# A recurrent layer's loads, decayed scores and state products re-arranged in a four-layer transformer kernel

## The chip, the core and the metric

The kernel runs on one core of a Trainium2 chip. The metric is device time in microseconds (us) for the whole program, which is all four layers in one launch. TensorE is called PE below, VectorE DVE, ScalarE ACT, GpSimd POOL, and SyncE (which here only issues transfers) SP.

## What is computed

Four layers act on 1024 latent tokens and 256 context tokens of width 1024. Layers 0 and 3 are windowed attention, layer 1 is a latent attention, and layer 2, the only one the change touches, is an mLSTM: a gated linear recurrence with a matrix state, run forwards and backwards, with 4 heads, keys of 128 and values of 256. In chunks of 128 tokens (10 chunks for each head and direction) the reference does:

```
c_new = a * c_prev + bb * c_loc
s_qk = einsum('bhctd,bhcsd->bhcts', q, k) * exp(log_d - m_t[..., None])
num = (einsum('bhcts,bhcsv->bhctv', s_qk, v)
       + a_t[..., None] * einsum('bhcvk,bhctk->bhctv', c_st, q))
den = sum(s_qk, axis=-1) + a_t * einsum('bhck,bhctk->bhct', n_st, q)
out = num / maximum(abs(den), exp(-m_t))[..., None]
```

The two directions are added, gated with a sigmoid and a silu, normalized by head and projected.

## The kernel before

Nearly all matrix products are made of 4-byte numbers split in two: `split` writes a rounded high half (`hi`, by ACT or DVE) and the rest (`lo`, by POOL or DVE), and a product then takes three PE instructions (high by high, high by low, low by high). A product whose operands are left as plain 4-byte floats is one instruction in the program; the trace shows two for it.

Layer 2 runs in stages (`layer_c`). First come the queries and keys of each head. Then twelve weight chunks of 256 columns are worked off in the loop over `c`. Chunks 0 to 3 give the values (`vd`), 4 to 7 the output gate (`sgd`), and 8 to 11 the second gate (`gzd`). The first eight chunks cover ten tiles of 128 tokens; the last four cover six, since the first four tiles of the second gate are put off (`late_z`). That makes 104 tiles. A tile is 24 products of 256 columns into a buffer `n`, which ACT, DVE or POOL empty into a small tile (`v` or `sg`) that SP stores.

Two generators are advanced inside this loop, so many steps for each tile. `gate_rows` computes the decay rows from the gates (on 36 partitions, a long chain on DVE, ACT and POOL) and stores them to `rmd` and `cqd`. `decays` then works through 24 groups of up to four chunks (4 heads, 2 directions): it loads five tiles a group (`e`, `a`, `q`, `st`, `kt`), and stores three results, the scaled keys `ked`, the decayed scores `gdd` and the scaled queries `qad`, up to 256 KB each.

After the loop come 40 steps, one for each head and chunk. Values of a head are loaded from `vd` as high and low halves (`rv`) by `load_head`; `load_decay` loads `ked`, `qad` and `gdd` two groups ahead and `group` splits them. In each step `state` makes the next state `cs` and `chunk` makes the output; the split of the state (`ch`, `cl`) lies between them. Between these products `fill(n)` puts `n` pieces of three products of `late_z`, 128 pieces in all. The tiles of the last head's steps feed the output projection (`wo`), whose weights are split in the last steps.

A scheduler with a simulated timeline sets the order of each engine's instructions; on the chip each engine and each queue, SP's too, takes its own in that order.

Of the kernel before, what the change touches and what calls it, by code (L numbers as in the profile page):

```python
# [9 lines left out]
F32 = mybir.dt.float32  # L10
F32R = mybir.dt.float32r
BF16 = mybir.dt.bfloat16
AF = mybir.ActivationFunctionType
ALU = mybir.AluOpType
# [9 lines left out]
NTL = NLAT // 128  # L24
# [7 lines left out]
def as32(ap):  # L32
    return ap.bitcast(F32)
# [31 lines left out]
class Dit:  # L65
# [1331 lines left out]
    def layer_c(self, i, hpool, hT, hs):  # L1397
        nc, ins, P = self.nc, self.ins, self.P
# [229 lines left out]
        rows = iter(())  # L1628
# [11 lines left out]
        def load_head(h):  # L1640
            sp = slots[h % 2]
            vv = []
            for x in range(2):
                v = sp.tile([128, NT, 258], F32R, name=f"rv{x}", bufs=1)
                nc.sync.dma_start(out=as32(v[:, :, 0:256]),
                                  in_=vd[x, :, h * 256:(h + 1) * 256].rearrange("(t p) d -> p t d", p=128))
                if x == 1:
                    nc.gpsimd.memset(as32(v[:, :, 256:258]), 0.0)
                else:
                    nc.gpsimd.memset(as32(v[:, :, 256:257]), 1.0)  # L1650
                    nc.gpsimd.memset(as32(v[:, :, 257:258]), -1.0)
                vv.append(v)
            hsum = sp.tile([128, NT, 256], F32, name="hsum", bufs=1)
            heads[h] = dict(v=vv, hsum=hsum, seen=set(), st=[None, None], nx=[None, None])

# [96 lines left out]
        dec = iter(())  # L1752
        for c in range(12):
            kind, h = c // 4, c % 4
            w = self.need(P["voz", c])
            tiles = [t for t in ORDER if kind < 2 or t >= 4]
            go = self.pacer(len(tiles), P["voz", c + 1] if c < 11 else None)
            if kind == 2:
                ghr = head_gain(wt, h)
            for t in tiles:  # L1760
                p = self.psn()
                self.proj_tok(p[:, 0:256], hT, t, w, 256)
                if pend and (c or t == 2):
                    kt_sT(*pend)
                    pend = None
                p = p[:, 0:256]
                go()
                r, cc = slice(t * 128, t * 128 + 128), slice(h * 256, h * 256 + 256)
                if kind == 0:
                    v = wt.tile([128, 2, 256], F32R, name="v", bufs=2)  # L1770
                    self.split(v[:, 0], v[:, 1], p, "act", "dve")
                    nc.sync.dma_start(out=vd[:, r, cc].rearrange("x p d -> p x d"), in_=as32(v))
                elif kind == 1:
                    s = wt.tile([128, 256], F32, name="sg", bufs=3)
                    nc.scalar.activation(out=s, in_=p, func=AF.Tanh, scale=0.5)
                    nc.vector.tensor_scalar(out=s, in0=s, scalar1=1.0, scalar2=0.5, op0=ALU.add, op1=ALU.mult)
                    nc.sync.dma_start(out=sgd[r, cc], in_=s)
                else:
                    gate_z(wt, p, t, h, ghr)
                next(rows, None)  # L1780
                for _ in range(2 if kind == 2 else 1):
                    next(dec, None)
            if c == 0:
                p1.release()
                gw = self.pool("gw", os_)
                rows = gate_rows()
            elif c == 6:
                for _ in rows:
                    pass
                gw.release()  # L1790
                pg = self.pool("pg", os_)
                dec = decays(pg)
# [30 lines left out]
        def fill(n):  # L1823
            for _ in range(n):
                next(zs, None)
# [3 lines left out]
        slots = [None, self.pool("slotb", os_)]  # L1829
        slots[0] = self.pool("slota", os_)  # L1830
        load_head(0)
        load_head(1)
        G, QA, KE = {}, {}, {}

        dec_t = {}
# [1 line left out]
        def load_decay(n):  # L1837
            if n < len(keys):
                h, d, c0 = keys[n]
                m = min(4, NT - c0)  # L1840
                dec_t[keys[n]] = []
                for src in (ked, qad, gdd):
                    x = p2.tile([128, 4, 128], F32, name="dT", bufs=9)
                    nc.sync.dma_start(out=x[:, 0:m].rearrange("p c t -> p (c t)"),
                                      in_=src[h, d, :, c0 * 128:(c0 + m) * 128])
                    dec_t[keys[n]].append(x)

        def group(h, d, c0):

            m = min(4, NT - c0)  # L1850
            load_decay(keys.index((h, d, c0)) + 2)
            ke, qa, dT = dec_t.pop((h, d, c0))
            for src, dic, nm in ((ke, KE, "k"), (qa, QA, "a"), (dT, G, "g")):
                hi = p2.tile([128, 4, 128], F32R, name=nm + "hi", bufs=3)
                lo = p2.tile([128, 4, 128], F32R, name=nm + "lo", bufs=3)
                self.split(hi[:, 0:m], lo[:, 0:m], src[:, 0:m], "act", "pool")
                for x in range(m):
                    dic[h, d, c0 + x] = (hi[:, x], lo[:, x])

        def state(h, c):  # L1860

            H = heads[h]
            cn = p2.tile([128, 2, 258], F32, name="cs", bufs=2)
            for d in range(2):
                v = [x[:, toks[d][c], :] for x in H["v"]]
                kh, kl = KE.pop((h, d, c))
                p = self.psn()[:, 0:258]
                self.mm(p, kh, v[0], True, False)
                self.mm(p, kh, v[1], False, False)
                self.mm(p, kl, v[0], False, True)  # L1870
                if c == 0:
                    nc.vector.tensor_copy(cn[:, d], p)
                else:
                    nc.vector.scalar_tensor_tensor(out=cn[:, d], in0=H["st"][0][:, d], in1=p, op0=ALU.mult, op1=ALU.add,
                                                   scalar=consts["abc"][:, 32 * d + h, c:c + 1])
            H["nx"] = (cn, p2.tile([128, 2, 258], F32R, name="ch", bufs=2), p2.tile([128, 2, 258], F32R, name="cl", bufs=2))

        def chunk(h, c):
            H = heads[h]
            w = self.psw()[:, :].rearrange("p (d n) -> p d n", d=2)  # L1880
            tk = [toks[d][c] for d in range(2)]
            for d in range(2):
                v = [x[:, tk[d], :] for x in H["v"]]
                gh, gl = G.pop((h, d, c))
                qh, ql = QA.pop((h, d, c))
                o = w[:, d, 0:258]
                self.mm(o, gh, v[0], True, False)
                self.mm(o, gh, v[1], False, False)
                self.mm(o, gl, v[0], False, c == 0)
                if c:  # L1890
                    _, ch_, cl_ = H["st"]
                    self.mm(o, qh, ch_[:, d], False, False)
                    self.mm(o, ql, ch_[:, d], False, False)
                    self.mm(o, qh, cl_[:, d], False, True)
            if c < NT - 1:
                cn, ch2, cl2 = H["st"] = H["nx"]
                self.split(ch2, cl2, cn, "act", "dve")
            dn = p2.tile([128, 2], F32, name="dn", bufs=3)
            nc.vector.tensor_reduce(out=dn, in_=w[:, :, 256:258], op=ALU.max, axis=AX.X)
            for d in range(2):  # L1900
                nc.vector.tensor_scalar(out=dn[:, d:d + 1], in0=dn[:, d:d + 1], scalar2=None, op0=ALU.max,
                                        scalar1=consts["colq"][:, c, 2 + d, h:h + 1])
            nc.vector.reciprocal(out=dn, in_=dn)
            if tk[0] in H["seen"]:
                for d in range(2):
                    hs_ = H["hsum"][:, tk[d]]
                    nc.vector.scalar_tensor_tensor(out=hs_, in0=w[:, d, 0:256], scalar=dn[:, d:d + 1], in1=hs_,
                                                   op0=ALU.mult, op1=ALU.add)
                    nc.sync.dma_start(out=gd[tk[d] * 128:tk[d] * 128 + 128, h * 256:(h + 1) * 256], in_=hs_)
            else:  # L1910
                for d in range(2):
                    nc.scalar.activation(out=H["hsum"][:, tk[d]], in_=w[:, d, 0:256], func=AF.Copy, scale=dn[:, d:d + 1])
                H["seen"].update(tk)
# [34 lines left out]
        for s, (h, c) in enumerate(steps):  # L1948
# [7 lines left out]
                            group(*key)  # L1956
            if c < NT - 1:
                state(h, c)
                fill(3)
            chunk(h, c)  # L1960
            fill(2)
            if c == 1 and h >= 1:
                if h < 3:
                    load_head(h + 1)
# [119 lines left out]
```

## Time and profile before

| | |
|---|---|
| median of three timed runs | 3041.59 us (3039.66 to 3044.81) |
| the profiled execution | 3034.74 us |
| its span, first to last instruction | 3033.0 us |
| PE busy over the span | 2820.0 us (93%) |
| mean granted PE clock | 0.973 |
| loop over the twelve chunks, first value store to last gate store | 1766.7 to 2137 us |
| 40 recurrent steps, first product to the output projection | 2149.2 to 2308 us |

PE's busy time counts a matmul from its start to its modelled end, and neighbours overlap, so a busy PE can still have room. The number of products in a stretch, times the distance between the starts of two that follow without a wait, says more.

### The profile page before, as it was taken

What the parts mean: (1) busy time and instruction counts of PE and PEld (TensorE: products, weight loads), DVE (VectorE), ACT (ScalarE), POOL (GpSimd) and SP (SyncE); (2) the same over time, 40 slices, a digit from 0 to 9 for tenths busy, and PEclk for the clock granted to TensorE, in tenths of its full rate; (3) what the DMA queues carried; (4) which work ended last, traced back from release to release, by engine and by line L of the source; (5) the groups of instructions that cost most, each with busy time, mean ns of one, the idle gap of its engine ahead of it and who ended that gap; (6) DMA issues with size and microseconds to landing.
All of it is one profiled execution on the core that took longest, in us unless ns stands there. A gap on an engine that the chain in (4) does not pass through costs nothing. (4 is left out here: it accounts for less than half of the span.)

```text
span 3033.0 us, 49504 instructions
## 1 busy us (share of the span) xinstructions
PE 2820.0 (93%) x17344; PEld 2448.9 (81%) x17344; DVE 1664.0 (55%) x3527; ACT 1273.3 (42%) x2685; POOL 1329.4 (44%) x1567
## 2 busy tenths in 40 slices
PE   6999999899989999999898999997798989999898
PEld 4888888678878788888787899997686778888777
DVE  5356666655422566666457645344587743666662
ACT  2245655543311455555333323232454422555662
POOL 4555565545661011000454232245685446655652
PEclk8999999999999999999999999998899999999999
DMA  8455463733355211111444354698886546434433
GB/s 266 150 160 165 131 178 109 227 122 125 95 189 170 58 39 36 33 37 33 137 146 124 115 165 137 202 295 270 258 257 229 186 127 185 125 113 139 150 94 112
DMA packets 460347, 446.36 MB, mean 147 GB/s; under 512 B 38882, under 2 KB 393722, under 8 KB 460098
## 3 DMA queue, kind: packets, MB, share of 16 engines
q1 hardware_dynamic: 455504, 440.40, 46.6%
q8 instruction: 138, 2.26, 0.3%
q10 hardware_dynamic: 4162, 2.14, 0.3%
q0 software_dynamic: 432, 0.66, 0.1%
q14 instruction: 111, 0.91, 0.1%
HBM read 308.19 MB, written 135.53 MB: 146 GB/s over the span
## 5 line engine op out<-in xcount | busy, mean ns | idle before, releaser
L104 DVE TENSOR_TENSOR pl<-n,ph 128x512 fp32r<-128x512 f32 x488 | 327.4, 686 | 139.2 <-ACT ph L95 121.1
L95 ACT ACTIVATE ph<-n 128x512 fp32r<-128x512 f32 x488 | 283.9, 596 | 213.3 <-PE n L90 168.7
L87 PE MATMUL n<-ph,v 128*128 128x256 f32 (+1 forms) x992 | 293.3, 338 | 21.0 <-ACT ph L95 15.2
L921 DVE CUSTOM_DVE_ANT_0 p<-w,mask,nsink 128x640 f32<-128x640 f32 (+2 forms) x288 | 225.0, 805 | 145.8 <-PE w L87 109.2
L87 PE MATMUL n<-wh,hh 128*128 128x256 f32 x960 | 277.8, 289 | 25.7 <-DVE sg L1748 19.7
L90 PE MATMUL n<-ident,p 128*128 128x128 f32 x1952 | 291.9, 276 | 4.3 <-ACT p L1291 1.4
L923 ACT ACTIVATE p<-p,nm 128x641 f32<-128x641 f32 (+2 forms) x288 | 220.7, 768 | 140.6 <-DVE nm L921 111.8
L87 PE MATMUL n<-wl,hh 128*128 128x256 f32 x960 | 274.9, 286 | 3.1 <-DVE wl L104 3.1
L87 PE MATMUL n<-wh,hl 128*128 128x256 f32 x960 | 274.4, 286 | 0.0
L90 PEld LDWEIGHTS n<-ident,p 128*128 128x128 f32 x1952 | 236.6, 142 | 38.5 <-ACT p L1288 2.8
L930 POOL TENSOR_SCALAR p<-p,rl 128x640 f32<-128x640 f32 (+2 forms) x288 | 211.0, 745 | 114.4 <-DVE rl L928 110.2
L87 PE MATMUL n<-pl,v 128*128 128x512 f32 (+1 forms) x656 | 239.1, 365 | 7.8 <-DVE pl L104 6.6
L1339 POOL TENSOR_TENSOR o<-o,z 128x256 f32<-128x256 f32 x40 | 30.3, 757 | 441.6 <-ACT o L1338 266.8
L87 PEld LDWEIGHTS n<-wh,hh 128*128 128x128 f32 x960 | 187.0, 195 | 29.8 <-DVE sg L1748 20.8
L87 PEld LDWEIGHTS n<-ph,v 128*128 128x128 f32 x992 | 175.1, 190 | 40.6 <-ACT ph L95 24.6
L87 PE MATMUL w<-ks,qT 128*128 128x256 f32 (+1 forms) x1088 | 198.3, 309 | 2.1 <-DVE nm L921 1.1
L87 PEld LDWEIGHTS n<-wl,hh 128*128 128x128 f32 x960 | 187.2, 195 | 3.9 <-DVE wl L104 3.8
L87 PEld LDWEIGHTS w<-ks,qT 128*128 128x128 f32 x1088 | 174.1, 189 | 18.8 <-DVE nm L921 4.6
L87 PEld LDWEIGHTS n<-wh,hl 128*128 128x128 f32 x960 | 186.9, 195 | 0.0
L104 POOL TENSOR_TENSOR wl<-raw,wh 128x1024 fp32r<-128x1024 f32 x42 | 105.8, 2524 | 152.4 <-DVE wh L97 142.2
L87 PEld LDWEIGHTS n<-pl,v 128*128 128x128 f32 x656 | 125.4, 191 | 26.9 <-DVE pl L104 18.4
L87 PE MATMUL n<-hh,wh 128*128 128x512 f32 (+1 forms) x336 | 124.4, 370 | 4.8 <-DVE mod L402 4.8
(349 smaller groups left out, 7449.0 us busy)
## 6 DMA issues: line engine op xcount, KB each, us to landing
raw<-in_l_w_ada_dram SPq DMA_DIRECT2D x96, 512.0 KB
raw<-in_l_w_in_dram SPq DMA_DIRECT2D x80, 512.0 KB
qT<-qd SPq DMA_DIRECT2D x576, 64.0 KB
raw<-in_l_w_out_dram SPq DMA_DIRECT2D x32, 512.0 KB
vd<-v SPq DMA_DIRECT2D x60, 256.0 KB
xd<-xt SPq DMA_DIRECT2D x30, 512.0 KB
od<-o SPq DMA_DIRECT2D x112, 128.0 KB
go<-od SPq DMA_DIRECT2D x28, 512.0 KB
```

The costliest lines, as they stand in the source:

```text
L87: self.nc.tensor.matmul(out, lhsT, rhs, start=start, stop=stop)
L90: self.nc.tensor.transpose(out, in_, self.ident)
L95: nc.scalar.activation(out=out, in_=in_, func=AF.Copy)
L104: e.tensor_tensor(out=lo, in0=src, in1=as32(hi), op=ALU.subtract)
L921: nc.vector.tensor_tensor_reduce(out=p[:, 0:n], in0=ps[:, s0:768], in1=mask[:, mo:mo + n], scale=1.0, scalar=sink, op0=ALU.add, op1=ALU.mi ...
L923: nc.scalar.activation(out=p[:, 0:n + 1], in_=p[:, 0:n + 1], func=AF.Exp, scale=-1.0, bias=nm[:, j:j + 1], accum_out=lsum[:, j:j + 1])
L930: nc.gpsimd.tensor_scalar(out=pr[y][:, 0:n], in0=pr[y][:, 0:n], scalar1=rl[:, y:y + 1], scalar2=0.5, op0=ALU.mult, op1=ALU.mult)
L1339: nc.gpsimd.tensor_tensor(out=o, in0=o, in1=z, op=ALU.mult)
```

## The change

It has five parts, all in layer 2. (1) `gate_rows` is advanced by two steps a tile and `decays` by one step throughout (before: one, and one or two); the scratch of `gate_rows` is freed after chunk 3 instead of 6, and `decays` begins from there. (2) The values of a head are loaded in pairs of tiles, ten transfers of 256 KB in the order in which the steps need them, in place of two of 1280 KB; the second head's are loaded at step 2. (3) 24 pieces of `late_z` stand ahead of the first step, then two pieces and one or two follow in each step (before: three and two). (4) The scaled queries are not split, and neither is the state; their product is one of plain 4-byte floats, in place of three. (5) The loaded tiles `dk`, `dq`, `dg` have buffers of their own (3, 4 and 3; before nine shared, `dT`), since `dq` is now held until its last chunk; `cs` has three.

```diff
@@ load_head
-                nc.sync.dma_start(out=as32(v[:, :, 0:256]),
-                                  in_=vd[x, :, h * 256:(h + 1) * 256].rearrange("(t p) d -> p t d", p=128))
...
+            for t in (NTL, 0, NTL - 2, 2, 4):
+                for x in range(2):
+                    nc.sync.dma_start(out=as32(vv[x][:, t:t + 2, 0:256]),
+                                      in_=vd[x, t * 128:(t + 2) * 128, h * 256:(h + 1) * 256]
+                                      .rearrange("(t p) d -> p t d", p=128))
@@ loop over the chunks
-                next(rows, None)
-                for _ in range(2 if kind == 2 else 1):
-                    next(dec, None)
+                for _ in range(2):
+                    next(rows, None)
+                next(dec, None)
...
-            elif c == 6:
+            elif c == 3:
...
         load_head(0)
-        load_head(1)
+        fill(24)
@@ load_decay
-                for src in (ked, qad, gdd):
-                    x = p2.tile([128, 4, 128], F32, name="dT", bufs=9)
+                for src, nm in ((ked, "dk"), (qad, "dq"), (gdd, "dg")):
+                    x = p2.tile([128, 4, 128], F32, name=nm, bufs=4 if nm == "dq" else 3)
@@ group
-            for src, dic, nm in ((ke, KE, "k"), (qa, QA, "a"), (dT, G, "g")):
+            for x in range(m):
+                QA[h, d, c0 + x] = qa[:, x]
+            for src, dic, nm in ((ke, KE, "k"), (dT, G, "g")):
@@ chunk
                 if c:
-                    _, ch_, cl_ = H["st"]
-                    self.mm(o, qh, ch_[:, d], False, False)
-                    self.mm(o, ql, ch_[:, d], False, False)
-                    self.mm(o, qh, cl_[:, d], False, True)
+                    self.mm(o, q, H["st"][:, d], False, True)
             if c < NT - 1:
-                cn, ch2, cl2 = H["st"] = H["nx"]
-                self.split(ch2, cl2, cn, "act", "dve")
+                H["st"] = H["nx"]
@@ steps
-                fill(3)
+                fill(2)
             chunk(h, c)
-            fill(2)
+            fill(1 + s % 2)
+            if s == 2:
+                load_head(1)
```

On SP, the decays' first loads stood behind the fifth output-gate store:

```order
L1777 DMA sgd_17452<-sg 128x256 x3
L1626 DMA cqd_17460<-colq 128x240
L1777 DMA sgd_17452<-sg 128x256
L1674 DMA colq<-cqd_17460 128x240
L1683 DMA e<-rmd_17456 128x512
```

With the change they stand behind the 28th of the 40 value stores:

```order
L1776 DMA vd_17451<-v 128x2x256 x5
L1626 DMA cqd_17460<-colq 128x240
L1776 DMA vd_17451<-v 128x2x256
L1678 DMA colq<-cqd_17460 128x240
L1687 DMA e<-rmd_17456 128x512
```

They moved ahead by 17 tiles. At the other end the last score store (`gdd`) stood behind 22 of the 24 second-gate stores of the loop, and now stands behind 11. From the first load to the last score store there were 57 tiles, now there are 63.

On SP again, at the turn to the steps, before the change: the second-gate stores end in the midst of the first loads of `load_decay`, and both heads' values follow.

```order
L1844 DMA dT<-qad_17457 128x512
L1750 DMA gzd_17453<-sg 128x256
L1844 DMA dT<-gdd_17458 128x512
L1844 DMA dT<-ked_17459 128x512
L1844 DMA dT<-qad_17457 128x512
L1844 DMA dT<-gdd_17458 128x512
L1844 DMA dT<-ked_17459 128x512
L1645 DMA rv_22869<-vd_17451 128x10x256
L1645 DMA rv_22873<-vd_17451 128x10x256
```

With the change:

```order
L1848 DMA dk<-ked_17459 128x256
L1848 DMA dg<-gdd_17458 128x256
L1754 DMA gzd_17453<-sg 128x256 x8
L162 DMA raw<-in_l_w_in_dram 128x4x256 x2
L1754 DMA gzd_17453<-sg 128x256
L1654 DMA rv_22869<-vd_17451 128x2x256
L1654 DMA rv_22872<-vd_17451 128x2x256
```

The decay tiles now go out while the last tiles of the loop are still made, and only the values are left behind the last gate store.

On PE, the turn from the loop to the steps, before (`wh_22327` is the loop's last weight chunk, `wh_22948` the first of `late_z`, `khi` the split keys):

```order
L87 MATMUL n_22820<-wl_22328,hh_16509 128x256
L87 MATMUL n_22820<-wh_22327,hl_16510 128x256
L87 MATMUL n_22934<-rv0_22869,khi_22903 128x258
L87 MATMUL n_22939<-rv0_22869,khi_22921 128x258
L87 MATMUL n_22959<-wh_22948,hh_16504 128x256
```

And with the change (`wh_22504` is the loop's last chunk, `wh_22887` the first of `late_z`; three of its tiles, 72 products, stand here before the first `rv0`):

```order
L87 MATMUL n_22820<-wl_22505,hh_16509 128x256
L87 MATMUL n_22820<-wh_22504,hl_16510 128x256
L87 MATMUL n_22898<-wh_22887,hh_16504 128x256
L87 MATMUL n_22928<-wh_22887,hh_16504 128x256
L87 MATMUL n_22958<-wh_22887,hh_16504 128x256
```

Before, PE's next product after the loop was one on the values, with all `late_z` products behind it. At the far end, 12 of the 40 steps stood on PE behind the last `late_z` product; with the change 7 do.

## Rows read from the trace of the kernel before

**Rows 1.** Busy time of the engines over the span, from the page's first part.
```profile
PE 2820.0 (93%) x17344; PEld 2448.9 (81%) x17344; DVE 1664.0 (55%) x3527; ACT 1273.3 (42%) x2685; POOL 1329.4 (44%) x1567
```

**Rows 2.** Windows: length, busy us (instructions) by engine, granted clock, DMA share, GB/s.
```profile
1929.00:2050.00 121.00, 116.12 (x962) 115.31 (x961) 58.18 (x104) 40.76 (x119) 51.27 (x40) 1.00 0.92 291
2050.00:2128.40 78.40, 58.93 (x437) 57.83 (x436) 31.80 (x69) 15.56 (x41) 45.62 (x47) 0.87 0.83 266
2128.40:2149.20 20.80, 0.00 (x0) 0.00 (x0) 7.21 (x9) 7.53 (x13) 17.05 (x21) 0.62 0.79 265
2149.20:2260.00 110.80, 106.43 (x855) 104.78 (x856) 83.90 (x226) 55.73 (x120) 77.90 (x73) 0.98 0.83 263
2260.00:2308.00 48.00, 31.47 (x200) 27.46 (x198) 45.19 (x106) 28.69 (x58) 40.48 (x28) 0.89 0.72 229
```

**Rows 3.** Timeline of PE at the turn: start, us, instruction [idle before, releaser].
```profile
2127.99 0.28 PE L87 MATMUL n<-wl,hh 128*128 128x256 f32 x1
2128.11 0.28 PE L87 MATMUL n<-wh,hl 128*128 128x256 f32 x1
2149.24 0.77 PE L87 MATMUL n<-rv,khi 128*128 128x258 f32 x2 [20.86 <-DMA rv<-vd]
2149.81 0.42 PE L87 MATMUL n<-wh,hh 128*128 128x256 f32 x1
```

**Rows 4.** Waits of PE from 2050 to 2129 us: total, times, longest.
```profile
PE n L87 <- DVE sg L1748: 19.5, 4, 8.5
```

**Rows 5.** Timeline of SP's issues: a value-store run, first decay load, last score store, values.
```profile
1863.25 14.29 SPq L1772 DMA_DIRECT2D vd<-v  x7
...
1929.10 0.43 SPq L1683 DMA_DIRECT2D e<-rmd  x1
...
2131.52 0.32 SPq L1730 DMA_DIRECT2D gdd<-e  x1
...
2141.18 9.37 SPq L1645 DMA_DIRECT2D rv<-vd  x4
```

**Rows 6.** Transfers from 1930 to 2050 us: GB/s in 40 slices, total, gate stores.
```profile
GB/s 227 282 92 223 378 343 350 301 241 363 377 361 261 282 259 192 282 371 270 193 383 334 289 281 350 296 290 327 303 286 360 379 329 158 314 304 322 201 292 287
DMA packets 33026, 35.20 MB, mean 293 GB/s; under 512 B 2769, under 2 KB 24694, under 8 KB 33014
...
sgd<-sg SPq DMA_DIRECT2D x35, 128.0 KB
```

**Rows 7.** Timeline of ACT, DVE and POOL at the turn: splits of the first late weights.
```profile
2130.72 1.06 ACT L95 ACTIVATE wh<-raw 128x1024 fp32r<-128x1024 f32 x1
...
2132.88 3.25 DVE L104 TENSOR_TENSOR wl<-raw,wh 128x1024 fp32r<-128x1024 f32 x1
...
2132.71 2.34 POOL L104 TENSOR_TENSOR wl<-raw,wh 128x1024 fp32r<-128x1024 f32 x1 [0.63 <-DVE wh L97]
```

**Rows 8.** Plain 4-byte products: weight loads on the timeline, then durations ns min/median/max.
```profile
1884.90 0.13 PEld L87 LDWEIGHTS n<-raw,cs 128*32 128x32 f32 x4
...
1885.11 0.13 PEld L87 LDWEIGHTS n<-raw,cs 128*32 128x32 f32 x4
...
L87 PE MATMUL n<-raw,cs x768: 379/379/637, 8.5 to 1885.3; 128*32 128x256 f32 x192
...
L87 PE MATMUL n<-wh,hh x960: 276/283/583, 1761.9 to 2256.4; 128*128 128x256 f32 x192
...
L87 PEld LDWEIGHTS n<-sel,part x192: 186/192/338, 14.0 to 1888.8; 128*128 128x128 f32 x192
```

**Rows 9.** Groups of instructions, 2149 to 2310 us: busy us, mean ns, idle before, releaser.
```profile
L104 DVE TENSOR_TENSOR cl<-cs,ch 128x516 fp32r<-128x516 f32 x36 | 37.9, 1052 | 1.0 <-ACT ch L95 0.4
...
L1874 DVE SCALAR_TENSOR_TENSOR cs<-cs,abc,n 128x258 f32<-128x258 f32 x64 | 29.3, 474 | 3.7 <-PE n L87 3.3
...
L95 ACT ACTIVATE ch<-cs 128x516 fp32r<-128x516 f32 x36 | 22.8, 632 | 24.9 <-PE w L87 10.5 <-DVE cs L1874 8.4 <-DVE dn L1899 4.7
...
L104 POOL TENSOR_TENSOR alo<-dT,ahi 128x512 fp32r<-128x512 f32 x14 | 20.8, 1487 | 0.0
```

**Rows 10.** Waits of SP's queue from 1950 to 2310 us: total, times, longest.
```profile
SPq L1844 <- POOL alo L104: 6.3, 11, 1.1
```

More of the change, by code (lines that the diff above doesn't have):

```diff
@@ L1862, in state @@
             H = heads[h]
-            cn = p2.tile([128, 2, 258], F32, name="cs", bufs=2)
+            cn = p2.tile([128, 2, 258], F32, name="cs", bufs=3)
             for d in range(2):
@@ L1873, in state @@
                 else:
-                    nc.vector.scalar_tensor_tensor(out=cn[:, d], in0=H["st"][0][:, d], in1=p, op0=ALU.mult, op1=ALU.add,
+                    nc.vector.scalar_tensor_tensor(out=cn[:, d], in0=H["st"][:, d], in1=p, op0=ALU.mult, op1=ALU.add,
                                                    scalar=consts["abc"][:, 32 * d + h, c:c + 1])
-            H["nx"] = (cn, p2.tile([128, 2, 258], F32R, name="ch", bufs=2), p2.tile([128, 2, 258], F32R, name="cl", bufs=2))
+            H["nx"] = cn
         def chunk(h, c):
@@ L1884, in chunk @@
                 gh, gl = G.pop((h, d, c))
-                qh, ql = QA.pop((h, d, c))
+                q = QA.pop((h, d, c))
                 o = w[:, d, 0:258]
```

## The prediction

> **What bounds the kernel now.** I read the page first, for the engines' shares: PE is busy 93% of the span [rows 1], so the work that counts is PE's. A stretch of layer 2 in which PE stands still is time to be had, and elsewhere a removed instruction of another engine is worth nothing. Next I read the timeline for what one product costs when nothing holds it: two that follow each other start 0.12 us apart [rows 3]. With that the windows tell how much PE lost in each stage, as the length less 0.12 us times the number of products [rows 2]:
>
> - 1929 to 2050 us (output gate, decays beside it): 962 products are 115.4 us of 121, lost 5.6. The transfer engines are 92% busy.
> - 2050 to 2128.4 (second gate, decays at two steps a tile): 437 products are 52.4 of 78.4, lost 26.0, at a granted clock of 0.87.
> - 2128.4 to 2149.2: no product at all, lost 20.8.
> - 2149.2 to 2260 (steps with late products): 855 products are 102.6 of 110.8, lost 8.2.
> - 2260 to 2308 (the last 12 steps, without any): 200 products are 24.0 of 48, lost 24.0. DVE is busy 45.2 us here and POOL 40.5.
>
> The waits say who held PE. From 2050 it is DVE's gate tile, 19.5 us in four waits [rows 4]: the buffers `n` are not emptied, since the engines that empty them are queued behind the decays, which wait for transfers. At the turn it is the value load, 20.86 us in one wait [rows 3], because SP issues it only at 2141.18, after the decays' last store at 2131.52 [rows 5]. So 84.6 us are lost in 379, and the change aims at four of the five stretches.
>
> **Decays begun earlier.** The first decay load goes out at 1929.10 now. With the change it stands behind the 28th value store, about the fifth of the seven stores that start at 1863.25 and last 14.3 us [rows 5], so near 1872, some 57 us sooner. What it needs is transfer room. From 1929 to 2128.4 the engines moved 291 x 121 + 266 x 78.4 = 56 MB [rows 2]. The new stretch, from first load to last score store, takes in 12 value stores of 256 KB, five more output-gate stores of 128 KB and about five more weight pieces of 512 KB, and drops 11 second-gate stores: 61 MB. At 291 GB/s that is 210 us, and at 291 / 0.92 = 316 GB/s 193 us, so the decays end between 2065 and 2082. PE alone would need 63 tiles of 24 products, 181 us. It may also run ahead of the emptying: in 1930 to 2050 it made 962 / 24 = 40 tiles while 35 gate tiles were stored [rows 2, 6], five ahead. So at 2065 to 2082 PE can stand at tile 96 of 104, and the last eight tiles take 23 us more: the loop ends between 2088 and 2105. Without any wait PE itself would end it at 2128.4 - 31.6 = 2096.8. Of the 31.6 us lost there now I therefore keep 10, which is the 5.6 of the first window taken over 200 us: **21 us gained**. The bounds are 31.6 (no wait left) and 12 (the 19.5 us of rows 4 come back earlier in the loop).
>
> The doubled `gate_rows` steps cost nothing where PE is five tiles ahead of DVE; DVE's work for them is the same, and only its place moves.
>
> The Trainium skill, in "DMA: Bandwidth & Descriptors", section "Where 436 GB/s comes from", puts the limit between the off-chip memory and one core at about 358 GB/s. By it the 61 MB would take 170 us, less than PE's 181, and nothing would be left of the loss; the trace's mean of 291 at a 0.92 share does not come near it, though single slices do. The sum goes by the mean.
>
> **The turn.** PE's queue had a product on the values in front. Now 72 late-gate products stand there, and they need only split weights. Today ACT starts that split at 2130.72, and DVE's low half, begun at 2132.88, lasts 3.25 us [rows 7], so it is done at 2136.1, 8.0 us after PE's last product. I take 8 us of standing still for 20.8: **12.8 us gained**. The two engines are then free of decays, so 4 us is the lower end (ACT's copy alone, 2.6 + 1.06 after the last product); 16 us is the upper, if the splits of keys and scores, loaded early now, stand ahead of the weights on ACT and POOL. The values, 2 x 256 KB behind the last gate store, must land within these 8 us and the 72 x 0.12 = 8.6 of the cover: today all four transfers, 5.1 MB, were issued at 2141.18 and the first product on them ran 8.1 us later [rows 3, 5], so a tenth of that amount is in time. If the cover is gone, the price is the same wait for less data, at most 8 us. The half clock after the pause (0.42 us for a product that takes 0.28 [rows 3]) stays.
>
> **The state's product.** There are 72 of them (9 chunks, 4 heads, 2 directions). The trace shows plain 4-byte products only with 32 columns of weights, four side by side: one such group follows the last after 0.21 us, and each product is two instructions [rows 8]. So 256 columns cost 0.42 to 0.43 us where three split products cost 0.36: 72 x 0.07 = **5 us lost**. From below, each half could cost one pass of 0.12 us (0.24, 8.6 us gained). From above, the loads could lie open: a full-width plain load lasts 192 ns at the median, two of them make 0.38 us more, 32 us lost. I take 5, since a split product's load lasts as long and is hidden behind 0.12 us.
>
> What goes away is 36 `ch` copies of 632 ns on ACT, 36 `cl` of 1052 ns on DVE and 24 `alo` on POOL (1487 ns for the 14 long ones) with as many copies on ACT [rows 9]. Where late products fill PE this is worth nothing. In the last steps it is.
>
> **The last steps.** Twelve steps stand behind the last late product now, seven with the change. At today's 2.0 us lost in a step (24.0 / 12) the loss becomes 14. Without `cl` a step has 1.05 us less on DVE, 7.4 us over seven, which would leave 7. I take 13, near the upper end, because POOL was nearly as full as DVE and the output weights' splits stay: **11 us gained** (bounds 10 and 17). The longer stretch with late products keeps its 8.2.
>
> **Sum.** 21 + 12.8 + 11 - 5 = 39.8 us. The profiled execution took 3034.7 us, 1.7 more than its span; it would take 2995. The timed median lies 6.9 above it, so I predict 3041.6 - 39.8 = **3002 us**.
>
> **Rivals.**
>
> - *The transfers have room.* The slices of rows 6 reach 383 GB/s, and if the new mix runs near that, the decays end before PE's own pace and all 31.6 us come back: 2991 us. Against it: a mean of 293 with few slices idle.
> - *The waits only move.* The transfers are as full from 1872 as they were from 1929, the value stores are twice as large as gate stores with two buffers instead of three, and `cqd` may be ready later than its place says; the loop then gives 12, and the turn, with splits queued ahead of the weights, 5: 39.8 - 9 - 7.8 = 23 us, 3019 us.
> - *The plain product's loads lie open.* Then it costs 32 and not 5, and 13 us are left: 3029 us. The steps would be PE's at 4.5 us and more instead of 3.9.
> - *Slower: SP held by `dq`.* A scaled-query tile is now held until its last chunk, and the load that takes its buffer waits on SP, in order, with `dk`, `dg`, weights and output stores behind it. Today SP's waits for such buffers are 6.3 us in 11, at most 1.1 [rows 10]. Twenty of the 24 loads have to take a used buffer. The gain is gone at 39.8 / 20 = 2.0 us of PE's time for each; at 2.5 us the kernel takes 3052 us. Against it: the hold is seen two groups ahead, some four steps of 3.9 us.
>
> **Chances.** Forecast 0.48 (its own range 2994 to 3010), room 0.12, moved waits 0.22, open loads 0.08, held queue 0.08; 0.02 that two of the losing cases come together and nothing changes. The range from 2984 to 3026 leaves out the held queue and most of the open loads. About 0.2%, 6 us, can be told from no change. Faster 0.88, same 0.04 (the last case and part of the open loads), slower 0.08.
>
> **What would show it.** The first decay load should stand near 1872 us and the last score store before 2085; PE's count from there to the end of the loop should come to 83 products in 10 us. At the turn PE should stand still for about 8 us, and start on late-gate products, not on `rv`. A product of `dq` and `cs` should hold PE for 0.43 us. The last seven steps should take 3.5 to 4.2 us each, with DVE no longer full. The prediction is wrong if PE waits for `v` or `sg` between 1872 and 2060 for over 20 us, if the first `rv` product waits for its transfer, or if SP's waits at `dq` show up again as PE's waits for split keys.

## Result and the profile after

The changed kernel takes 3024.0 us (median of five runs, 3013.6 to 3029.2) where the kernel before took 3039.7 beside it: a ratio of 0.9939, 95% interval 0.9913 to 0.9965. Measured once more it gave 0.9938 (0.9919 to 0.9957). So about 18 us are gained by both ratios, not 39.8 (the medians lie 15.7 and 18.0 us apart). The first profiled execution has a span of 3013.8 us against 3033.0. Its page differs little in the shares; PE has 72 instructions less:

```profile
PE 2825.1 (94%) x17272; PEld 2450.8 (81%) x17272; DVE 1631.5 (54%) x3491; ACT 1246.6 (41%) x2625; POOL 1297.6 (43%) x1543
```

To see where the time went I cut the recurrent layer of every trace at the same products: the 1st, 961st and 1921st product of the loop over weight chunks (where values, output gate and second gate begin), its last one, the first product on the values, and the first of the output projection. Each entry is the difference of two start times on PE's timeline, so what the layers ahead of the loop take is left out; its first product stands at 1757.1 to 1769.4 us in the sixteen profiles, though no edit changes the code ahead of it.

| us | values | output gate | second gate | turn | steps to the output projection | sum |
|---|---|---|---|---|---|---|
| before | 147.6 | 123.1 | 95.5 | 21.1 | 161.3 | 548.7 |
| changed | 164.1 | 122.4 | 90.0 | 14.3 | 146.8 | 537.6 |
| changed, second profile | 159.8 | 121.8 | 90.0 | 14.3 | 145.9 | 531.8 |

The loop, forecast 21 us shorter, is 5 to 10 us longer in these profiles (366.2 before, 371.6 and 376.5 after), because the values' chunks lost 12 us or more and the second gate won only 5.5. Turn and steps won 21.3, forecast 18.8. The windows show the same. First the value chunks of before, a row not shown yet (columns as in [rows 2]):

```profile
1761.94:1909.54 147.60, 143.10 (x1164) 136.59 (x1162) 62.48 (x118) 39.62 (x65) 33.07 (x21) 1.00 0.45 139
```

Then the changed kernel from the values to the output projection, and the stretch from the first decay load to the last score store:

```profile
1757.14:1921.22 164.08, 153.47 (x1175) 146.08 (x1174) 69.96 (x153) 46.87 (x84) 43.19 (x30) 0.94 0.56 174
1921.22:2043.60 122.38, 117.53 (x963) 115.76 (x962) 54.85 (x104) 40.16 (x115) 50.08 (x36) 1.00 0.91 284
2043.60:2133.72 90.12, 76.74 (x578) 75.07 (x576) 37.10 (x64) 16.39 (x39) 56.58 (x54) 0.92 0.70 221
2133.72:2147.94 14.22, 10.66 (x75) 10.29 (x73) 4.55 (x5) 2.10 (x4) 6.23 (x11) 0.88 0.70 222
2147.94:2254.16 106.22, 104.35 (x782) 100.42 (x781) 68.50 (x229) 38.69 (x82) 59.46 (x61) 1.00 0.85 272
2254.16:2294.72 40.56, 25.86 (x143) 22.07 (x141) 25.56 (x69) 17.48 (x35) 22.80 (x16) 0.83 0.72 235
...
1880.69:2097.47 216.78, 199.05 (x1592) 195.06 (x1590) 102.98 (x193) 59.87 (x168) 99.03 (x79) 0.97 0.89 279
```

The value chunks hold nearly the same products as before, but last 16 us longer at a granted clock of 0.94. The timelines of PE, DVE, SP and POOL show the first of two new stops, behind the 23rd of the 40 value tiles (start, us, engine, line; code lines stand 4 lower in the file than before from here on):

```profile
1849.42 1.07 PE L87 MATMUL n<-raw,cs 128*32 128x256 f32 x16
1855.94 0.45 PE L90 MATMUL n<-ident,s 128*128 128x128 f32 x1 [5.45 <-DVE v L104]
...
1856.95 0.41 PE L87 MATMUL n<-wl,hh 128*128 128x256 f32 x1
1857.16 0.41 PE L87 MATMUL n<-wh,hl 128*128 128x256 f32 x1
...
1854.77 0.69 DVE L97 CAST wh<-raw 128x1024 fp32r<-128x1024 f32 x1 [7.18 <-DMA raw<-in_l_w_in_dram]
1855.38 0.75 DVE L104 TENSOR_TENSOR v<-n,v 128x256 fp32r<-128x256 f32 x2
...
1850.81 0.37 SPq L162 DMA_DIRECT2D raw<-in_l_w_in_dram  x1
...
1847.27 1.16 POOL L1610 MEMSET s<- 36x1280 f32 x1 [14.50 <-ACT v L95]
1848.40 2.38 POOL L104 TENSOR_TENSOR wl<-raw,wh 128x1024 fp32r<-128x1024 f32 x1
```

PE waits 5.45 us for a value split on DVE. DVE itself stands at the split of the next weight piece, whose load went out only at 1850.81, and the value splits are queued behind it. The load follows POOL's low half of the piece before (`wl`), which ends at 1850.78 and stands behind the clearing of a row tile (L1610). After the pause two products start 0.21 us apart instead of 0.12 until 1863.4, the lower of the clock's two levels (1.2 GHz); the granted clock is 0.54 there:

```profile
1857.00:1863.00 6.00, 6.00 (x31) 5.83 (x30) 0.30 (x2) 0.77 (x2) 1.47 (x2) 0.54 0.88 256
```

Second, behind the 34th value tile, a modulation piece (`part`, `gc`) meets the decays' first steps (L1723) on DVE:

```profile
1898.37 0.61 PE L87 MATMUL n<-sel,part 128*128 128x2 f32 x4 [1.56 <-DVE part L388]
1901.49 0.38 PE L90 MATMUL n<-ident,gc 128*16 128x128 f32 x1 [2.51 <-DVE gc L413]
...
1896.96 0.69 DVE L1723 SCALAR_TENSOR_TENSOR e<-st,e 128x512 f32<-128x512 f32 x1 [1.65 <-POOL e L1719]
...
1899.21 2.22 DVE L413 TENSOR_TENSOR gc<-mod,cols 128x8 f32<-128x8 f32 x2
```

The decays moved as they were meant to, though not as far. SP's timeline, beside [rows 5]:

```profile
1878.54 0.34 SPq L1626 DMA_DIRECT2D cqd<-colq  x1
...
1880.69 0.42 SPq L1687 DMA_DIRECT2D e<-rmd  x1
...
2097.47 0.37 SPq L1734 DMA_DIRECT2D gdd<-e  x1
...
2139.62 0.60 SPq L1654 DMA_DIRECT2D rv<-vd  x1
```

They start 48 us sooner and end 34 us sooner (2131.52 before), after 217 us at 279 GB/s, 60.5 MB; counted from the loop's first product, which itself stands 4.8 us sooner, it is 44 and 29. At their end PE had 234 products of the loop still to do, which are 28 us, and they took 36 (the last one ran at 2133.60). Of the 21 us that the second gate lost (90.0 less 576 products at 0.12), 13 came ahead of that moment and 8 behind it; in the second profile it was 12 and 9. Ahead of it, from 2044 to 2098, DVE waits for the decays' row loads (the first line); behind it PE and others wait for other things (the rest, 2098 to 2134):

```profile
DVE e L1716 <- DMA e<-rmd: 11.7, 4, 4.6
...
ACT sg L1751 <- DMA gzd<-sg: 10.0, 4, 4.0
ACT khi L95 <- DMA dk<-ked: 7.3, 2, 7.1
...
POOL ghr L1745 <- DMA ghr<-in_l_g_head_dram: 4.9, 2, 3.8
PE n L87 <- DVE sg L1752: 4.6, 2, 2.8
```

At the turn the order is as forecast, late-gate products first and no wait at the first product on the values, beside [rows 3]:

```profile
2133.60 0.28 PE L87 MATMUL n<-wh,hl 128*128 128x256 f32 x1
2135.35 0.63 PE L87 MATMUL n<-wh,hh 128*128 128x256 f32 x3 [1.47 <-ACT wh L95]
2138.07 0.39 PE L87 MATMUL n<-wl,hh 128*128 128x256 f32 x1 [2.09 <-DVE wl L104]
...
2147.94 0.40 PE L87 MATMUL n<-rv,khi 128*128 128x258 f32 x2
```

And the plain product of state and query, in the last steps:

```profile
2254.89 0.60 PE L87 MATMUL w<-cs,dq 128*128 128x258 f32 x2
2255.13 0.59 PE L87 MATMUL w<-rv,ghi 128*128 128x258 f32 x2
2255.55 0.28 PE L87 MATMUL w<-rv,glo 128*128 128x258 f32 x1
```

From the product's start to the one after the next pair are 0.66 us; the pair alone takes 0.24, so the plain product holds PE 0.42 us.

### The profile page after: what moved, and what is told of

Same layout as the page of the kernel before. It is cut to its first block, busy times and chain, and to the rows that moved or that the text cites. A ratio compares the mean times of both kernels' runs of the same rounds, so it can differ in the third digit from the quotient of the medians.

```text
span 3013.8 us, 49186 instructions
## 1 busy us (share of the span) xinstructions
PE 2825.1 (94%) x17272; PEld 2450.8 (81%) x17272; DVE 1631.5 (54%) x3491; ACT 1246.6 (41%) x2625; POOL 1297.6 (43%) x1543
## 5 line engine op out<-in xcount | busy, mean ns | idle before, releaser
L921 DVE CUSTOM_DVE_ANT_0 p<-w,mask,nsink 128x640 f32<-128x640 f32 (+2 forms) x288 | 225.0, 806 | 145.1 <-PE w L87 106.4
L87 PE MATMUL n<-hh,wh 128*128 128x512 f32 (+1 forms) x336 | 123.6, 368 | 5.9 <-DVE mod L402 5.9
```

The source lines that it names most:

```text
L87: self.nc.tensor.matmul(out, lhsT, rhs, start=start, stop=stop)
L921: nc.vector.tensor_tensor_reduce(out=p[:, 0:n], in0=ps[:, s0:768], in1=mask[:, mo:mo + n], scale=1.0, scalar=sink, op0=ALU.add, op1=ALU.mi ...
```

## Experiments

All are compared with the kernel before, timed beside them on the same chip. Theory A is that the row steps at double rate stand ahead of the weight splits and cost what the earlier decays win; theory B is the prediction's own, 21 us from the loop; theory C that the transfers' total sets the loop.

**The changed kernel again.** Without an edit:

> The changed kernel itself once more, to see what of its first profile returns. Theory A: the value chunks (first product of the loop to the 960th) take 160 to 164 us again, the second gate 89 to 91, the loop 371 to 377, and the ratio to the kernel before is 0.993 to 0.996. Theory B (the first profile was a chance result): the loop takes 345 to 360.

The values take 159.8 us, the second gate 90.0, the loop 371.6 (its row in the table above), so the loss in the values returns.

**The loop's edit alone, and everything but it.** The first puts this into the kernel before, the second takes it out of the changed kernel:

```diff
-                next(rows, None)
-                for _ in range(2 if kind == 2 else 1):
-                    next(dec, None)
+                for _ in range(2):
+                    next(rows, None)
+                next(dec, None)
...
-            elif c == 6:
+            elif c == 3:
```

> The kernel before with the loop's edit alone: two gate-row steps a tile, decays begun behind the fourth weight chunk, one decay step a tile. Theory A (the doubled row steps stand ahead of the weight splits, and what the earlier decays win is given back in the values' chunks): the loop, from its first product to its last, takes 370 to 380 us instead of 366.2, and the time is 3035 to 3050. Theory B (the prediction's own: the loop gains 21, and the one profiled pair is a chance result): 345 us and about 3019. Theory C (the transfers' total sets the loop, wherever the decays stand): 366 us and 3036 to 3043.

> The changed kernel with the loop's edit undone: row steps, decay steps and their first chunk as before, everything else as changed. Theory A: the loop takes 366 us again, the turn and the steps keep their gain of 21, and the time is 3010 to 3020, not above the changed kernel's 3024. Theory B: the loop's 21 us are missing, so 3040 or more beside 3024 of the changed kernel. Theory C: the same as the changed kernel, 3021 to 3027.

| us | median | ratio (95%) | values | second gate | turn | steps | sum |
|---|---|---|---|---|---|---|---|
| loop alone | 3036.5 | 0.9990 (0.9978 to 1.0003) | 160.1 | 90.7 | 14.6 | 159.8 | 547.1 |
| all but the loop | 3023.4 | 0.9956 (0.9940 to 0.9972) | 152.2 | 99.3 | 19.4 | 150.2 | 543.2 |

Alone the loop's edit gives nothing that can be told: 12 us lost in the values, 5 won in the second gate, 6.5 at the turn. The rest alone gives 13 us. On top of the rest, which is the changed kernel, the loop's edit gives some 5 us by the ratios, and their intervals overlap. Theory B falls. A did not hold for the second run either: it said 366 us for the loop and a time of 3010 to 3020. The unedited loop took 373.7 us there, against 366.2 in the profile of before, so two profiles of the same loop's code differ by up to 7.5 us; 3 us of that arise at the sixth value tile, ahead of all that is changed, in some profiles and not in others (the first of the changed kernel has them, the second hasn't). The values' 157 us and more with doubled rows, against 148 to 154 without, stands in all the runs below. C's times came in both runs, but its loop of 366 did not; the later runs, with the same transfers, have loops of 356.0 to 376.5 us, so the transfers' total does not set it.

**One row step a tile, slow and fast decays.** In the changed kernel the row steps go back to one a tile and the decays begin behind the fifth chunk; the second run also has two decay steps a tile in the second gate.

```diff
-                for _ in range(2):
-                    next(rows, None)
-                next(dec, None)
+                next(rows, None)
+                for _ in range(2 if kind == 2 else 1):
+                    next(dec, None)
...
-            elif c == 3:
+            elif c == 4:
```

> The changed kernel with one gate-row step a tile, as before, and the decays begun behind the fifth chunk (the 36 row steps are then done), one decay step a tile. Theory A (the row steps at double rate are the loss): the stop of 5 us with a half clock behind it in the values' chunks is gone, the loop takes 355 to 366 us, and the time is 3005 to 3015. Theory C (transfers): the loop stays at 370 or more and the time at 3021 to 3027. If the decays' early start itself is the loss, it lies between e2 and the changed kernel.

> The changed kernel with one gate-row step a tile and decays behind the fifth chunk, as in the run with single row steps, but two decay steps a tile in the second gate, so that the decays end at the same tile as in the changed kernel. Theory A: value chunks of 148 to 154 us instead of 164, second gate 88 to 92, the turn 14 to 16 with the values in time, so 8 to 12 us less than the changed kernel, 3010 to 3016. If the transfers set the loop, the 10 us come back as second gate and turn: the same as the changed kernel.

| us | median | ratio (95%) | values | second gate | turn | steps | sum |
|---|---|---|---|---|---|---|---|
| slow decays | 3028.7 | 0.9967 (0.9954 to 0.9979) | 153.7 | 88.6 | 33.2 | 151.6 | 547.6 |
| fast decays | 3027.2 | 0.9969 (0.9955 to 0.9983) | 149.1 | 88.0 | 29.5 | 149.2 | 537.8 |

The values' loss is gone, as theory A says. But A gave 3005 to 3016 for the two, and by the ratios they are 8 to 9 us slower than the changed kernel. The turn took it all. With fast decays (PE, ACT and SP):

```profile
2149.45 0.77 PE L87 MATMUL n<-rv,khi 128*128 128x258 f32 x2 [11.32 <-issue]
...
2148.72 0.63 ACT L95 ACTIVATE khi<-dk 128x512 fp32r<-128x512 f32 x1 [10.17 <-DMA dk<-ked]
...
1929.95 0.43 SPq L1687 DMA_DIRECT2D e<-rmd  x1
...
2134.05 0.32 SPq L1734 DMA_DIRECT2D gdd<-e  x1
```

The first decay load went out at 1929.95, as before the change, though the code begins the decays two chunks sooner: they need the row chain's last store (`cqd`, at 1927.25), and at one step a tile that comes no earlier. They end at 2134.05; only then can the keys' loads and splits follow, and PE, done with the loop at 2119.9 and with the 72 late products at 2138, waits 11 us for them. So doubling the row steps is what moves the decays: it costs time in the values and saves it at the turn.

**Where the row chain stops the values.** Four runs. An own buffer for the second stored row tile; the same with the rows' two stores issued from ACT; the decays put one chunk later with the rows still doubled; and three row steps for two tiles.

```diff
-                n32 = row("s3")
+                n32 = row("s2" if x else "s3")
...
-                nc.sync.dma_start(out=rmd[x], in_=n32[R])
+                nc.scalar.dma_start(out=rmd[x], in_=n32[R])
...
+            elif c == 4:
                 pg = self.pool("pg", os_)
                 dec = decays(pg)
...
-                for _ in range(2):
+                for _ in range(1 + tiles.index(t) % 2):
                     next(rows, None)
```

> The changed kernel with another buffer for the second of the two stored row tiles, so that its clearing on POOL need not wait for the first one's store. If that wait is what keeps the weight's low half, and with it the weight buffer and the next load, the stop of 6.5 us at the 32nd value tile is gone and the half clock behind it: value chunks 153 to 157 instead of 164, and 6 to 10 us off the time, 3014 to 3018. If the weight load is late for the transfers' sake, the stop stays and the time is that of the changed kernel, 3021 to 3027.

> The run with an own row buffer, with the two stores of the rows issued from ACT instead of SP, so that the weight load of the 24th value tile is not queued on SP behind a store that waits for ACT's rows. If that queue makes the weight late, its load goes out 3 us or more sooner, the stop at the 24th tile falls from 5.5 to 2 us or less, and the value chunks take 155 to 157 instead of 160. If the load is bound otherwise (its buffer, the transfers), nothing moves.

> The changed kernel with the row steps at double rate as changed, but the decays begun one chunk later, behind the fifth, so that none stands beside a value tile. If the row chain alone stops the value chunks, they take 160 us as before. If the second stop (at the 34th value tile, where a modulation piece meets the decays' first steps on DVE) is the decays', only the first stop of about 5.5 us at the 24th tile stays, and the value chunks take 153 to 156.

> The changed kernel with three gate-row steps for two tiles instead of four; the decays still begin behind the fourth chunk. Theory A (the row chain's queueing stops the value chunks): its stops move away from the modulation pieces, value chunks 152 to 157 us instead of 160 to 164, first decay load some 20 us later (about 1905) and the last score store near 2115; the loop 364 to 369 and the time 3012 to 3018. If the decays' own start beside the values is what costs, the values stay at 160.

| us | median | ratio (95%) | values | second gate | turn | steps | sum |
|---|---|---|---|---|---|---|---|
| own row buffer | 3018.7 | 0.9945 (0.9925 to 0.9965) | 160.1 | 90.7 | 14.3 | 145.5 | 532.0 |
| and stores from ACT | 3014.4 | 0.9919 (0.9904 to 0.9934) | 157.3 | 91.0 | 14.3 | 146.9 | 530.1 |
| decays later in the code | 3021.1 | 0.9936 (0.9919 to 0.9954) | 161.7 | 87.8 | 14.3 | 149.1 | 537.3 |
| three steps for two tiles | 3005.3 | 0.9894 (0.9881 to 0.9908) | 154.0 | 86.8 | 14.9 | 145.1 | 524.0 |

The buffer alone changed nothing: the weight load left the wait behind POOL's clearing and stood on SP behind the rows' second store instead, and PE's stop became several waits for value splits on DVE, which for their part waited for ACT's high halves, first behind the row copies and at last behind a value store:

```profile
1854.76 0.32 SPq L1614 DMA_DIRECT2D rmd<-s  x1
1855.17 0.38 SPq L162 DMA_DIRECT2D raw<-in_l_w_in_dram  x1
...
1858.12 0.42 DVE L104 TENSOR_TENSOR v<-n,v 128x256 fp32r<-128x256 f32 x1 [2.56 <-ACT v L95]
...
1858.69 0.30 PE L90 MATMUL n<-ident,s 128*128 128x128 f32 x1 [2.00 <-DVE v L104]
1862.03 0.58 PE L87 MATMUL n<-wh,hh 128*128 128x256 f32 x1 [2.86 <-DVE v L104]
```

With the stores on ACT the load goes out 1.8 us sooner after the loop's first product than in the second profile of the changed kernel, not 3 or more, and the stop falls from 5.1 us to 3.6, not to 2 (the first line is the second profile's, the other this run's):

```profile
1860.89 0.45 PE L90 MATMUL n<-ident,s 128*128 128x128 f32 x1 [5.11 <-DVE v L104]
1857.02 0.30 PE L90 MATMUL n<-ident,s 128*128 128x128 f32 x1 [3.56 <-DVE v L104]
```

What remains is on DVE: four row steps of 1.48 us stand in one piece ahead of the weight split, and the load follows POOL's low half at once:

```profile
1846.77 1.48 DVE L1593 SCALAR_TENSOR_TENSOR s<-s,s 36x1280 f32<-36x1280 f32 x1
1848.18 0.41 DVE L104 TENSOR_TENSOR v<-n,v 128x256 fp32r<-128x256 f32 x1
1848.51 0.68 DVE L97 CAST wh<-raw 128x1024 fp32r<-128x1024 f32 x1
...
1849.27 2.40 POOL L104 TENSOR_TENSOR wl<-raw,wh 128x1024 fp32r<-128x1024 f32 x1 [2.54 <-DVE wh L97]
...
1851.70 0.37 SPq L162 DMA_DIRECT2D raw<-in_l_w_in_dram  x1
```

So the same piece is held by several queues, and freeing one of them hands it to the next. The run with the decays later in the code tells nothing of its question: their first load went out 122 us after the loop's first product, as in the changed kernel (124 and 120), again right behind the row chain's last store. That the second stop comes from the decays is therefore argued from its rows, not shown by a run. But the traces bound the decays' part. Cut the values' last 17 tiles once more, at the 552nd product (the last one ahead of the first stop, and behind the 3 us that come and go), the 721st and the 816th (the last one ahead of the second stop):

| us | 552nd to 721st | 721st to 816th | 816th to 961st |
|---|---|---|---|
| one step a tile (4 profiles) | 24.9 to 27.9 | 12.6 | 21.1 |
| two steps (10 profiles) | 31.5 to 34.7 | 12.6 | 24.1 to 24.7 |
| three for two tiles (2 profiles) | 28.1 | 14.5 | 19.3 |

In all ten profiles with two steps the 721st product starts before any engine has done a step of the decays. So the 7 us lost up to there, on the mean, cannot be theirs and go with the doubled rows; 3 to 4 us at most are left for the decays. Three steps for two tiles win at both ends: the values take 154 us, and the decays, begun at 1902.62, need 205 us and not 217, with 58.7 MB at 286 GB/s; most value stores are through by then. They end at 2107.84, in time for the turn. This version beats both kernels, 32 us below the one before and below the 3012 to 3018 that were expected.

**The second gate after the decays.** Three runs: the first groups' splits on ACT ordered behind the loop's last gate tile; two buffers for the head gain `ghr`, with and without that order; and, last, these two with three row steps for two tiles.

```diff
-            ghr = wk.tile([128, 256], F32, name="ghr", bufs=1)
+            ghr = wk.tile([128, 256], F32, name="ghr", bufs=2)
...
-                self.split(hi[:, 0:m], lo[:, 0:m], src[:, 0:m], "act", "pool")
+                with self.tc.issue_after(lt.ins):
+                    self.split(hi[:, 0:m], lo[:, 0:m], src[:, 0:m], "act", "pool")
```

> The changed kernel with the first groups' splits on ACT ordered behind the loop's last gate tile (ACT's order alone, no wait added). If the second gate's 21 us of loss are in part those splits, which wait for their loads in front of three gate tiles, the second gate takes 84 to 86 us instead of 90, and the time falls by 3 to 6, if the splits are still in time behind the 72 late products; if they are late then, the turn grows by as much and the time stays. If the loss is all the decays', nothing moves.

> The changed kernel with two buffers for the gate's head gain instead of one. In the run with the splits held, POOL waited 10.3 us for that load at the heads' turns after the last score store, with three gate tiles behind it. If this load is what keeps the second gate at 90 us though the decays end 35 us before it, the second gate takes 82 to 86 us and the time falls by 4 to 8, to about 3012. If the transfers or the decays keep it, it stays at 89 to 91 and nothing moves.

> Two buffers for the head gain and the first groups' splits on ACT behind the loop's last gate tile. If the two waits stand in parallel (either alone is replaced by the other), this gives more than both runs apart: second gate 78 to 82 us, 8 to 12 us less than the changed kernel. If they add up, 82 to 86. If neither counts, 90.

> Three row steps for two tiles, two buffers for the head gain, splits held behind the last gate tile: the three together. If each gives what its theory says, the loop takes 355 to 360 us and the time is 3005 to 3012, below both kernels. If the first product on the values cannot come before 386 us from the loop's beginning, because the decays end later, the turn grows by what the loop gains, and the time is the changed kernel's.

| us | median | ratio (95%) | values | second gate | turn | steps | sum |
|---|---|---|---|---|---|---|---|
| splits held | 3016.2 | 0.9931 (0.9912 to 0.9949) | 160.1 | 90.2 | 14.3 | 146.3 | 532.8 |
| two gain buffers | 3012.9 | 0.9918 (0.9905 to 0.9931) | 160.2 | 85.5 | 14.9 | 143.1 | 526.5 |
| both | 3012.3 | 0.9919 (0.9907 to 0.9932) | 160.0 | 86.1 | 15.1 | 143.1 | 526.1 |
| both, three steps for two tiles | 3007.4 | 0.9900 (0.9887 to 0.9913) | 154.1 | 79.4 | 15.8 | 147.3 | 519.1 |

With the splits held, POOL's wait for the gain load came in their place, at the heads' turns with the gate tiles behind it:

```profile
POOL sg L1753 <- DVE sg L1752: 11.6, 5, 5.5
POOL ghr L1745 <- DMA ghr<-in_l_g_head_dram: 10.3, 2, 6.6
```

A second buffer takes 4.5 us off the second gate, as was expected; holding the splits gives nothing, alone or with it. So a part of the stage's loss never was the decays': a gain of 1 KB a row, fetched only when the head before it was done. All together give the shortest second gate and a loop of 356.0 us, as expected (355 to 360), but a time that cannot be told from three steps for two tiles alone.

**The state's splits.** The changed kernel with state and scaled queries split as before (the `ch`, `cl`, `ahi`, `alo` lines of the diff put back).

> The changed kernel with the state and the scaled queries split again, as before (three products of 0.12 us for one plain one). By the prediction's terms the products give back 72 x 0.07 = 5 us, and the last steps lose 7.4 us, since DVE has its 36 low halves of 1.05 us again: 3026. If the plain product's price is all that counts: 3019. If the last steps are bound by DVE and POOL as before: 3031 or more.

It took 3028.7 us, 0.9970 (0.9957 to 0.9983). Values 160.5, second gate 89.1, turn 14.3 as in the changed kernel; the steps 153.8 instead of 146.8 and 145.9. Up to the last late product it is no slower (104.8 us, against 106.1 and 105.0); all of it lies in the stretch behind: 49.0 us, where the changed kernel has 40.7 and 40.9 and the kernel before 53.9. That stretch holds the outputs of 12 steps there, of 9 in the changed kernel and of 14 before, so it is not a step that became shorter: 4.1, 4.5 and 3.9 us for an output. The upper of the three expectations, with the last steps held by the splits, is nearest.

## Why the prediction was wrong

The time came into the range, but by 0.6% instead of 1.3%, because of one term.

**Decays begun earlier (forecast 21 gained): the step that failed.** Two sentences of it did not hold. The first is that the doubled `gate_rows` steps "cost nothing where PE is five tiles ahead of DVE". They stand in the value chunks, where PE did wait for DVE, and the working had looked at the output gate's window. There they cost some 10 us of 160: profiles with one step a tile have 148 to 154 us in the values, all with two 157 to 164, and three for two tiles 154. Some 7 of the 10 are lost before the decays do anything. The second is "Of the 31.6 us lost there now I therefore keep 10". By the same count 28 are kept: 7 in the output gate and 21 of 26 in the second gate, 13 of these while the decays still run, which ended later than worked out, and 8 behind them, where the waits name the gain load, the gate stores and the key loads. That all 26 were the decays' was read into a wait that only names DVE's gate tile [rows 4]; behind DVE stood several causes, the decays one of them. A second buffer for the gain alone takes 4.5 us off.

The transfers' amount held, 60.5 MB found for 61, but not their time, 217 us for 193 to 210. The working took the 291 GB/s of its first window, while its own 56 MB in 199.4 us are 281; the trace before has 277 GB/s from the first decay load to the last store, the changed one 279. The Trainium skill, in "DMA: Bandwidth & Descriptors", section "Where 436 GB/s comes from", puts the limit between the off-chip memory and one core at about 358 GB/s, by which that amount would pass in an estimated 170 us. The trace's 279 GB/s does not come near it, and the measurement decides.

**The first load** stood at 1880.7, not 1872 (123.6 us after the loop's first product, forecast 110), for it waits for the row chain's last store, a risk named under the rival of moved waits only. That rival's time (3019) is near by luck: it gave the loop 12 and the turn 5, and the loop gave nothing and the turn 15.

**The signs of being wrong** did not come. The first product on the values did not wait, and PE waited 6.1 us for `v` or `sg` from 1872 to 2060, under the 20 that were set, but the first stop, in which it waited 5.45 for `v`, ended at 1856, ahead of that window.

**The turn (forecast 12.8 gained)** was right in its order and better in size: 21.1 us with no product became 14.3 with 72 in them, which are 8.6, so 5.7 us are lost and 15.4 gained. The weight split did not stand behind decays any more: 10.8 us are lost where only the loop's edit is missing (19.4 less 8.6). So the loop's edit pays some 5 us here, which it does not pay in the loop.

**The state's product** was right: 0.42 us for 0.43, the loads hidden. The Trainium skill, in "FP8 and Floating Point Precision", section "TensorE Precision Notes", counts four passes for a true 4-byte product; an estimate by it, 4 x 0.12, is 0.48, and the row's 0.42 is somewhat less.

**The last steps** (11 gained, 5 lost by the product, 6 net): the steps from the first value product on are 14.5 us shorter, of which 8.6 are the 72 products done at the turn, so 5.9 net. That this fits is luck in part, for the place is another. With 0.12 us a product and 0.42 a plain one taken off, the stretch behind the last late product lost 25.6 us before and loses 20.7 now, 5 less and not 11, and an output takes 4.5 us there, above the 3.5 to 4.2 forecast; DVE is no longer full (25.6 us of 40.6). The other 5 come in the steps with late products, which lost 8.0 and lose 2.8, where the forecast kept 8.2. The run that puts the splits back says as much: its steps take 7 to 8 us more in all, with the outputs of three more behind the last late product, at 4.1 us each. SP was hardly held by `dq`; its waits from 2100 to 2295 us at the line that issues these loads, for the products that read them, are 2.8 us:

```profile
SPq L1848 <- PE w L87: 2.8, 3, 2.0
```

## What to carry to other kernels

Before filler work is made denser, look at the tiles where it will stand, not at those where it stands now: here a chain of small steps on DVE, POOL, ACT and SP delayed one weight load, and behind its stop of 5.5 us 24 products started 0.21 us apart, which cost 2.2 us more. A phase that is begun earlier in code starts when its last input is stored; find that store before counting the gain. And a stage whose worst wait is shortened keeps the next ones: name them from the trace before taking the whole loss as the gain, and search for the rate in between, which won more than either end.

## What the runs showed that I had not expected

Of the full-width plain product's 0.42 us only 0.24 show up to the next product's start; the other 0.18 come in the distance between the two products behind it, so the price is read over three starts. And the 24 decay groups take 217 us when begun at 1881, among the value stores, 205 when begun at 1902, and 202 before the change, begun at 1929. The rates are near each other (279, 286 and 277 GB/s); the bytes that pass in these stretches are 60.5, 58.7 and 56.1 MB.
